# Dilated attention: four heads' scores in one piece, with the transposes and values of older steps, between the products of a fused three-block kernel

## The chip, the cores and the metric

One core of one Trainium2 chip runs the whole program. The time is device time in microseconds of one execution; the runs of a kernel are given by their median. TensorE (PE, its weight loads PEld), VectorE (DVE), ScalarE (ACT), GpSimd (POOL) and SyncE (SP, which issues the DMAs) each have their own instruction stream and wait for one another by semaphores.

## The reference, cut to what matters

Three transformer-like blocks follow one another on 512 tokens of 1024 features, all in float32: a block with RWKV-7 and differential attention between two gated feed-forwards, a second block with a pooling mixer and a dilated attention, and a third with mLSTM, sparse attention and a convolutional feed-forward. The change touches only the dilated attention of the second block. For each of three dilations (1, 4 and 16, numbered 0 to 2) and sixteen heads of 64 features:

```
s = q @ k.T * 0.125 - slope(dilation, head) * distance     # only keys in the window
m, z = max(s), sum(exp(s - m));  o = exp(s - m) @ v
out = merge of the three (o, m, z) by their maxima, divided by the merged z
out = out * silu(x @ w_gate), then @ w_out, residual, layer norm
```

In dilation 0 a query tile of 128 tokens sees its own and the preceding 128 keys (the first tile only its own). In the others the tokens are permuted, and each tile of 128 sees its own 128 keys.

## The kernel before, in words

Products with weights are done in three parts for accuracy: weights and activations are split into a high and a low float32r part, and `mm3` (L591) issues low x high, high x low, high x high (L594 to L596). The weights come as a stream of blocks of 128 x 512 (`Stream`, L152): SP loads a block, ScalarE casts its high part (L183), VectorE subtracts for the low part (L184). There are seven buffers for prepared blocks.

`dilated_heads` (L1500) loops over dilation `g` and a group `q` of four heads. Each turn computes keys and queries, `kq`: four columns of 8 k-steps, 512 tokens wide (`gemm_fg`, 32 steps of one `mm3`), and then values, `v`: four tiles of tokens, 8 k-steps of 256 columns each (`gemm_tg`, 16 steps of two `mm3`). These products go to three accumulator banks of PSUM (`acc`) and are copied out by ScalarE (L1517, L1523). In the first turn there is nothing beside them.

The attention of the group just projected is a generator, `dil_unit` (L1535), whose pieces end at a `yield`. `weave` (L145) runs the next turn's 48 product steps and lets the unit go one piece further after every `1 / pace` of them. So a unit's instructions stand between the next group's products on TensorE: `DIL_PACE` 0.5 gives its 24 pieces one place after every second step. The last unit stands beside the first 32 steps of the gate products (`gt`, `GATE_PACE` 0.8).

A unit has eight steps: four query tiles `i` times two pairs of heads `hp`. For each, three pieces:

- `scores` (L1553): for the two heads `b` of the pair a matmul of 64 rows (head `b` on partitions 64b to 64b+63) into a PSUM bank of its own (L1562); VectorE adds the bias and reduces the maximum (`mx`) on its way to `ds` (L1563), ScalarE exponentiates and sums (L1564).
- `turn` (L1567): TensorE transposes the exponentials in blocks of 128 x 128 into a third bank (L1574), and ScalarE or VectorE copies them to `dpT` (L933, L931).
- `values` (L1579): matmuls of 128 rows and 64 columns into the one bank `dO` (L1589); after two tiles `merge` (L1593) copies them out (dilation 0) or merges them with `dl_acc` by VectorE and POOL.

The order issued is scores of step n+1, turn of n, values of n. Scores, transposes and the like share four PSUM banks (`aux`) in turn. A float32 matmul leaves two records on TensorE for scores and values, and one for a transpose. At its end a dilation-0 unit is written to memory and read back in the permuted order by two DMAs of SP. The instructions of each engine are placed by the framework's scheduler, which keeps the issued order unless an instruction's buffers fall free earlier or later.

Of the kernel before, what the change touches and what calls it, by code (L numbers as in the profile page):

```python
# [9 lines left out]
F32 = mybir.dt.float32  # L10
F32R = mybir.dt.float32r
AF = mybir.ActivationFunctionType
ALU = mybir.AluOpType
# [3 lines left out]
P = 128  # L17
T = 512
# [45 lines left out]
LA_MORE = 6  # L64
WO_MORE = 3
KQ_FS = 4
DIL_PACE = 0.5
GATE_PACE = 0.8
GATE_LAG = 6
MEMSET = 8  # L70
PREP_PACE = 1.5
# [45 lines left out]
def chain(*gens):  # L117
    for g in gens:
        yield from g
# [25 lines left out]
def weave(main, other, n):  # L145

    fill(main, other, n)
    for _ in other:
        pass
# [234 lines left out]
class DiffAttention:  # L384
# [36 lines left out]
    def attend(self, d):  # L421
# [11 lines left out]
        def scores(n, m):  # L433
            i, h = todo[n]
            id, N = f"{d}_{i}_{h}", (i + 1) * P
            if m == 0:
# [77 lines left out]
class Build:  # L514
# [985 lines left out]
    def dilated_heads(self, u, up, accs, last):  # L1500
        nc, tc = self.nc, self.tc
        S = nc.scalar
        with tc.tile_pool(name="dil", bufs=1) as pd, tc.tile_pool(name="dild", bufs=4, space=bass.MemoryType.DRAM) as pdr:
            c = self.load_consts(pd, "cst2b", ["rel0", "rel1", "rel2"], self.ext["cst2"][:, 64:])
            perm = lambda a: a.rearrange("q (j p) -> q p j", p=4)

            def reorder(k, src, dst):
                nc.gpsimd.tensor_copy(dst[:, k].rearrange("q (p j) -> q p j", p=4), perm(src[:, k]))

            unit = None  # L1510
            for g in range(3):
                for q in range(4):
                    kq = pd.tile([P, 4, T], F32, tag="kq", bufs=2, name=f"kq{g}_{q}")
                    vt = pd.tile([P, 4, 256], F32, tag="vt", bufs=2, name=f"vt{g}_{q}")

                    def evac(n, ps, c0, c1, kq=kq):
                        S.copy(kq[:, n, c0:c1], ps)  # L1517

                    h0 = g * D + q * 256
                    cols = [("w_kv_2", h0), ("w_kv_2", h0 + P), ("w_in_b_2", h0), ("w_in_b_2", h0 + P)]  # L1520
                    ug = up if g else u
                    kqs = self.gemm_fg(ug, KD, cols, evac, fs=KQ_FS if g == q == 0 else 0, uid=f"kq{g}{q}")
                    vs = self.gemm_tg(ug, KD, "w_kv_2", 3 * D + h0, 256, lambda t, n, ps, vt=vt: S.copy(vt[:, t], ps), f"v{g}{q}")  # L1523
                    if not unit:
                        for _ in kqs:
                            pass
                        self.psum(**MIX_BANKS)
                        unit = iter(())
                        pairs = [(k, a, b) for a, b in ((u.hi, up.hi), (u.lo, up.lo)) for k in range(KD)]
                        self.steps(0, REORDER_GAP, [lambda x=x: reorder(*x) for x in pairs])  # L1530
                    weave(chain(kqs, vs), unit, DIL_PACE)
                    unit = self.dil_unit(g, q, kq, vt, accs[q], c, pd, pdr)
            weave(last, unit, GATE_PACE)

    def dil_unit(self, g, q, kq, vt, acc, c, pd, pdr):  # L1535
        nc = self.nc
        V, S, G = nc.vector, nc.scalar, nc.gpsimd
        mm = nc.tensor.matmul
        W = 256 if g == 0 else P
        rel = c[f"rel{g}"]  # L1540
        bias = pd.tile([P, 4, 256], F32, tag="dbias", bufs=2, name=f"dbias{g}_{q}")
        for h in range(4):
            slope = 2.0 ** (-8.0 * (g * 16 + q * 4 + h + 1) / 48.0)
            G.tensor_scalar(bias[:, h, :W], rel, -8.0 * slope, 0.0, op0=ALU.mult, op1=ALU.add)
        mx = pd.tile([P, 4, 4], F32, tag="dmx", bufs=2, name=f"dmx{g}_{q}")
        zz = pd.tile([P, 4, 4], F32, tag="dzz", bufs=2, name=f"dzz{g}_{q}")
        nat = None
        if g == 0:
            nat = pd.tile([P, 4, 264], F32, tag="dnat", bufs=1, name=f"dnat{q}")
        steps = [(i, hp) for i in range(4) for hp in range(2)]  # L1550
        st, po = {}, {}

        def scores(i, hp):  # L1553
            id = f"{g}{q}_{i}{hp}"
            N = P if (g or i == 0) else 256
            ks = slice(P * i, P * (i + 1)) if N == P else slice(P * (i - 1), P * (i + 1))
            s = pd.tile([P, 2, 256], F32, tag="ds", bufs=2, name=f"ds{id}")
            for b in range(2):
                h = 2 * hp + b
                ps = self.aux(f"dS{id}_{b}", N)  # L1560
                bs = slice(64 * b, 64 * b + 64)
                mm(ps, kq[bs, 2 + hp, P * i : P * (i + 1)], kq[bs, hp, ks], start=True, stop=True)  # L1562
                V.tensor_tensor_reduce(s[:, b, :N], ps, bias[:, h, W - N : W], -0.125, 3e38, ALU.add, ALU.min, mx[:, i, h : h + 1])  # L1563
                S.activation(s[:, b, :N], s[:, b, :N], AF.Exp, bias=mx[:, i, h : h + 1], scale=-1.0, accum_out=zz[:, i, h : h + 1])  # L1564
            st[i, hp] = (s, N)

        def turn(i, hp):  # L1567
            id = f"{g}{q}_{i}{hp}"
            s, N = st[i, hp]
            nb = N // P  # L1570
            pt = self.aux(f"dP{id}", 2 * N)
            for b in range(2):
                for j in range(nb):
                    nc.tensor.transpose(pt[:, (b * nb + j) * P : (b * nb + j + 1) * P], s[:, b, j * P : (j + 1) * P], self.ident)  # L1574
            pT = pd.tile([P, 512], F32, tag="dpT", bufs=2, name=f"dpT{id}")
            self.copy(i + hp, pT[:, : 2 * N], pt)
            st[i, hp] = pT, N

        def values(i, hp):  # L1579
            id = f"{g}{q}_{i}{hp}"  # L1580
            pT, N = st.pop((i, hp))
            nb = N // P
            if (i % 2, hp) == (0, 0):
                po[0] = self.po([P, 2, 4, 64], f"dO{id}")
            for b in range(2):
                h = 2 * hp + b
                for j in range(nb):
                    kt = i if N == P else i - 1 + j
                    mm(po[0][:, i % 2, h], pT[:, (b * nb + j) * P : (b * nb + j + 1) * P], vt[:, kt, h * 64 : (h + 1) * 64], start=j == 0, stop=j == nb - 1)  # L1589
            if (i % 2, hp) == (1, 1):  # L1590
                merge(i - 1, po[0])

        def merge(i0, po):  # L1593
            sl = slice(i0, i0 + 2)
            if g == 0:
                S.copy(nat[:, sl, :256], po.rearrange("a i h e -> a i (h e)"))
                return
            id = f"{g}{q}_{i0}"
            M, Z = acc[:, sl, 256:260], acc[:, sl, 260:264]
            t = pd.tile([P, 3, 2, 4], F32, tag="dmt", bufs=2, name=f"dmt{id}")  # L1600
            V.tensor_tensor(t[:, 0], M, mx[:, sl], op=ALU.min)
            V.tensor_tensor(t[:, 1], t[:, 0], M, op=ALU.subtract)
            V.tensor_tensor(t[:, 2], t[:, 0], mx[:, sl], op=ALU.subtract)
            S.activation(t[:, 1:], t[:, 1:], AF.Exp)
            V.tensor_copy(M, t[:, 0])
            V.tensor_tensor(Z, Z, t[:, 1], op=ALU.mult)
            V.tensor_tensor(zz[:, sl], zz[:, sl], t[:, 2], op=ALU.mult)
            V.tensor_tensor(Z, Z, zz[:, sl], op=ALU.add)
            for j in range(2):
                o = acc[:, i0 + j, :256].rearrange("a (h e) -> a h e", h=4)  # L1610
                bc = lambda a: a.unsqueeze(2).to_broadcast([P, 4, 64])
                V.tensor_tensor(o, o, bc(t[:, 1, j]), op=ALU.mult)
                w = pd.tile([P, 4, 64], F32, tag="dmw", bufs=2, name=f"dmw{id}_{j}")
                V.tensor_tensor(w, po[:, j], bc(t[:, 2, j]), op=ALU.mult)
                G.tensor_tensor(o, o, w, op=ALU.add)

        scores(*steps[0])
        yield
        for n, s in enumerate(steps):
            if n + 1 < len(steps):  # L1620
                scores(*steps[n + 1])
                yield
            turn(*s)
            yield
            values(*s)
            yield
        if g == 0:
            G.tensor_copy(nat[:, :, 256:260], mx)
            G.tensor_copy(nat[:, :, 260:264], zz)
            dr = pdr.tile([T, 264], F32, tag="dperm", name=f"dperm{q}")  # L1630
            nc.sync.dma_start(dr.rearrange("(i a) c -> a i c", a=P), nat)
            nc.sync.dma_start(acc, dr.rearrange("(j p) c -> j p c", p=4))

    def bias_rows(self, pool):

# [565 lines left out]
```

## Time and profile before

| | us |
|---|---|
| median of 3 runs (2902.62 to 2905.06) | 2902.79 |
| the profiled execution | 2904.9 |
| its span, first to last instruction | 2903.1 |
| TensorE busy | 2841.8 |
| VectorE / ScalarE / POOL busy | 1550.4 / 1211.3 / 431.5 |
| scores L1562 with the first unit's, from 1578.8 to | 2136.0 |

In a row of the profile `dS<-kq` names what is written and read, `64*128 64x256` the rows and columns of the array and then the shape, and "idle ... <-X" the time in which the engine stood still and what ended it. A matmul's recorded length holds its passage through the array, so the next one starts before it ends; what a matmul costs is read from start to start. A timeline joins equal neighbours of one engine to one row with a count; it starts at the first and is as long as to the last one's end.

### The profile page before, as it was taken

The page shows a single profiled execution, that of the slowest core. Times are in us where ns is not written, and L with a number is a line of the kernel's source. Part 1 is how long each engine was busy: PE and PEld are TensorE (multiplying, and loading weights), DVE is VectorE, ACT ScalarE, POOL GpSimd, SP SyncE. Part 2 cuts the span into 40 slices and gives each one's busy share as a digit, 9 for nine tenths or more (in the row PEclk, how much of TensorE's full clock was granted, in tenths as well). Part 3 has the DMA queues.
Part 4 walks back from the last instruction along what each step waited for, and adds up shares of the span by engine and source line. Part 5 has one row for each costly group of instructions (what it writes and reads, how often), then busy time and mean ns, then how long its engine had stood idle before and what let it go on. Part 6 is the DMA issues. An engine that isn't in the chain of part 4 may idle for free.

```text
span 2903.1 us, 44178 instructions
## 1 busy us (share of the span) xinstructions
PE 2841.8 (98%) x16743; PEld 2384.7 (82%) x16743; DVE 1550.4 (53%) x3365; ACT 1211.3 (42%) x2524; POOL 431.5 (15%) x509
## 2 busy tenths in 40 slices
PE   8999989999999999999999999999999999999998
PEld 7888887868887888888888888888899777888887
DVE  5443276565665443265446333444466895577742
ACT  5333263233334333243334444444474546554431
POOL 2110041010023110112304000111004023200001
PEclk9999999999999999999999999999999999999999
DMA  4333351101023333333242323222232421133332
GB/s 141 98 95 97 96 164 37 39 28 37 30 71 89 98 97 96 91 106 92 87 131 62 99 77 96 66 81 73 66 100 73 107 70 60 58 109 95 98 95 73
DMA packets 136141, 245.31 MB, mean 84 GB/s; under 512 B 15064, under 2 KB 22232, under 8 KB 135800
## 3 DMA queue, kind: packets, MB, share of 16 engines
q1 hardware_dynamic: 135928, 242.49, 27.6%
q8 instruction: 131, 2.15, 0.3%
q14 instruction: 82, 0.67, 0.1%
HBM read 235.75 MB, written 6.68 MB: 84 GB/s over the span
## 4 chain that ended last, share of the span: by engine, by line
PE 88%; DVE 6%; POOL 2%; ACT 2%; issue 1%; DMA 0%; SPq 0%; POOLq 0%; DVEq 0%; ACTq 0%
PE f_gu L594 5%; PE f_gu L596 5%; PE f_gu L595 5%; PE kq L594 3%; PE kq L595 3%; PE kq L596 3%; PE cf L594 3%; PE cf L595 3%; PE cf L596 3%; PE f L594 3%; PE f L596 3%; PE f L595 3%; PE v L594 2%; PE dO L1589 2%; PE v L595 2%; PE v L596 2%
## 5 line engine op out<-in xcount | busy, mean ns | idle before, releaser
L184 DVE TENSOR_TENSOR wlo<-wraw,whi 128x512 fp32r<-128x512 f32 (+1 forms) x858 | 627.2, 736 | 626.0 <-ACT whi L183 624.4
L183 ACT CAST whi<-wraw 128x512 fp32r<-128x512 f32 (+1 forms) x858 | 528.2, 619 | 897.1 <-PE f_gu L596 275.0
L594 PE MATMUL f<-f_ah,wlo 128*128 128x512 f32 (+1 forms) x440 | 153.8, 350 | 1.1 <-DVE wlo L184 1.1
L596 PE MATMUL f<-f_ah,whi 128*128 128x512 f32 (+1 forms) x440 | 153.4, 349 | 0.0
L595 PE MATMUL f<-f_al,whi 128*128 128x512 f32 (+1 forms) x440 | 153.4, 349 | 0.0
L594 PE MATMUL f_gu<-n_uh,wlo 128*128 128x512 f32 (+1 forms) x376 | 143.1, 381 | 9.2 <-ACT n_uh L788 8.2
L595 PE MATMUL f_gu<-n_ul,whi 128*128 128x512 f32 (+1 forms) x376 | 142.8, 380 | 0.0
L596 PE MATMUL f_gu<-n_uh,whi 128*128 128x512 f32 (+1 forms) x376 | 142.6, 379 | 0.0
L594 PE MATMUL f_gu<-won_uh,wlo 128*128 128x512 f32 (+1 forms) x376 | 142.2, 378 | 0.0
L596 PE MATMUL f_gu<-won_uh,whi 128*128 128x512 f32 (+1 forms) x376 | 142.0, 378 | 0.0
L595 PE MATMUL f_gu<-won_ul,whi 128*128 128x512 f32 (+1 forms) x376 | 141.8, 377 | 0.0
L594 PE MATMUL cf<-w3on_uh,wlo 128*128 128x512 f32 (+1 forms) x376 | 141.6, 377 | 0.0
L595 PE MATMUL cf<-w3on_ul,whi 128*128 128x512 f32 (+1 forms) x376 | 141.3, 376 | 0.0
L596 PE MATMUL cf<-w3on_uh,whi 128*128 128x512 f32 (+1 forms) x376 | 141.3, 376 | 0.0
L1563 DVE CUSTOM_DVE_ANT_0 ds<-dS,dbias 128x128 f32<-128x128 f32 (+1 forms) x192 | 54.9, 321 | 135.6 <-PE dS L1562 135.6
L1564 ACT ACTIVATE ds<-ds,dmx 128x128 f32<-128x128 f32 (+1 forms) x192 | 80.9, 422 | 100.7 <-DVE dmx L1563 100.3
L594 PE MATMUL kq<-dl_uh,wlo 128*128 128x512 f32 x256 | 112.6, 440 | 0.0
L595 PE MATMUL kq<-dl_ul,whi 128*128 128x512 f32 x256 | 100.7, 393 | 0.0
L596 PE MATMUL kq<-dl_uh,whi 128*128 128x512 f32 x256 | 100.2, 391 | 0.0
L594 PEld LDWEIGHTS f<-f_ah,wlo 128*128 128x128 f32 x440 | 82.7, 188 | 13.3 <-DVE wlo L184 1.3
L596 PEld LDWEIGHTS f<-f_ah,whi 128*128 128x128 f32 x440 | 82.7, 188 | 12.2
L595 PEld LDWEIGHTS f<-f_al,whi 128*128 128x128 f32 x440 | 82.7, 188 | 12.2
(831 smaller groups left out, 7606.0 us busy)
## 6 DMA issues: line engine op xcount, KB each, us to landing
wraw<-w SPq DMA_DIRECT2D x856, 256.0 KB, 2.6
dperm<-dnat SPq DMA_DIRECT2D x4, 528.0 KB, 3.9
dl_acc<-dperm SPq DMA_DIRECT2D x4, 528.0 KB, 3.6
x<-x SPq DMA_DIRECT2D x4, 512.0 KB, 6.9
xd<-x SPq DMA_DIRECT2D x8, 256.0 KB, 3.3
x<-xd SPq DMA_DIRECT2D x8, 256.0 KB, 3.6
toep<-rvd SPq DMA_DIRECT2D x8, 256.0 KB, 4.9
out<-x SPq DMA_DIRECT2D x16, 128.0 KB, 1.8
```

The costliest lines, as they stand in the source:

```text
L183: b.nc.scalar.copy(hi[:, s], raw[:, s])
L184: b.nc.vector.tensor_tensor(lo[:, s], raw[:, s], hi[:, s].bitcast(F32), op=ALU.subtract)
L594: mm(ps, a[1], b[0], start=start, stop=False)
L595: mm(ps, a[0], b[1], start=False, stop=False)
L596: mm(ps, a[0], b[0], start=False, stop=stop)
L1563: V.tensor_tensor_reduce(s[:, b, :N], ps, bias[:, h, W - N : W], -0.125, 3e38, ALU.add, ALU.min, mx[:, i, h : h + 1])
L1564: S.activation(s[:, b, :N], s[:, b, :N], AF.Exp, bias=mx[:, i, h : h + 1], scale=-1.0, accum_out=zz[:, i, h : h + 1])
L1589: mm(po[0][:, i % 2, h], pT[:, (b * nb + j) * P : (b * nb + j + 1) * P], vt[:, kt, h * 64 : (h + 1) * 64], start=j == 0, stop=j == nb - 1)
```

## The change

`scores` now takes all four heads of its tiles: one query tile in dilation 0, two in the others, so that a unit has 4 or 2 steps. Head `b` of both pairs and both tiles goes to bank `b`, at the columns that `slots` gives; all matmuls come first, then the reductions and exponentials. `turn` transposes a step's exponentials into two banks, one copied by ScalarE and one by VectorE. A piece consists of `turn` of step n-1, `values` of step n-2 and `scores` of step n, without a product in between: 5 pieces a unit in dilation 0, 3 in the others. A unit's last values, and in dilation 0 its write to memory, are handed on (`before`) and run in the next unit's first piece, ahead of its scores. The pace is set so that the pieces come after steps 10, 19, 28, 37 and 46 of 48, or 16, 31 and 46; beside the gates after 7, 14, 21 and, for the last values, 28 of 32. The buffers `ds` and `dpT` hold 2 x 512 columns in place of 2 x 256 and 512.

```diff
-DIL_PACE = 0.5
-GATE_PACE = 0.8
+DIL_STEPS = 46
+GATE_STEPS = 28
...
-                    weave(chain(kqs, vs), unit, DIL_PACE)
-                    unit = self.dil_unit(g, q, kq, vt, accs[q], c, pd, pdr)
-            weave(last, unit, GATE_PACE)
+                    weave(chain(kqs, vs), unit, pace)
+                    unit = self.dil_unit(g, q, kq, vt, accs[q], c, pd, pdr, before)
+                    pace = (3 if g else 5) / DIL_STEPS
+            weave(last, chain(unit, (f() for f in before)), 4 / GATE_STEPS)
...
-        steps = [(i, hp) for i in range(4) for hp in range(2)]
+        steps = [(i,) for i in range(4)] if g == 0 else [(0, 1), (2, 3)]
...
+        def slots(tiles):
+            return [(i, hp, (hp * len(tiles) + j) * 512 // (2 * len(tiles))) for hp in range(2) for j, i in enumerate(tiles)]
+
+        def scores(n):
+            tiles = steps[n]
...
+            N = P if (g or n == 0) else 256
+            s = pd.tile([P, 2, 512], F32, tag="ds", bufs=2, name=f"ds{id}")
+            ps = [self.aux(f"dS{id}_{b}") for b in range(2)]
+            for i, hp, a in slots(tiles):
+                ks = slice(P * i, P * (i + 1)) if N == P else slice(P * (i - 1), P * (i + 1))
+                for b in range(2):
+                    bs = slice(64 * b, 64 * b + 64)
+                    mm(ps[b][:, a : a + N], kq[bs, 2 + hp, P * i : P * (i + 1)], kq[bs, hp, ks], start=True, stop=True)
             for b in range(2):
...
+                for i, hp, a in slots(tiles):
+                    h = 2 * hp + b
+                    o = s[:, b, a : a + N]
+                    V.tensor_tensor_reduce(o, ps[b][:, a : a + N], bias[:, h, W - N : W], -0.125, 3e38, ALU.add, ALU.min, mx[:, i, h : h + 1])
+                    S.activation(o, o, AF.Exp, bias=mx[:, i, h : h + 1], scale=-1.0, accum_out=zz[:, i, h : h + 1])
...
+        def turn(n):
...
+            pT = pd.tile([P, 2, 512], F32, tag="dpT", bufs=2, name=f"dpT{id}")
+            for b in range(2):
+                pt = self.aux(f"dP{id}_{b}")
+                for _, _, a in slots(steps[n]):
+                    for c0 in range(a, a + N, P):
+                        nc.tensor.transpose(pt[:, c0 : c0 + P], s[:, b, c0 : c0 + P], self.ident)
+                if N * 2 * len(steps[n]) == 512:
+                    self.copy(b, pT[:, b], pt)
...
+        for n in range(L + 1):
+            if n:
+                turn(n - 1)
+            if n >= 2:
+                values(n - 2)
+            if not n and before:
+                before[0]()
+            if n < L:
+                scores(n)
+            if n == L:
+                before[:] = [finish]
             yield
```

## Rows read from the trace of the kernel before

**Rows 1.** The page, first part: busy us (share of the span) and instructions.
```profile
PE 2841.8 (98%) x16743; PEld 2384.7 (82%) x16743; DVE 1550.4 (53%) x3365; ACT 1211.3 (42%) x2524; POOL 431.5 (15%) x509
```
**Rows 2.** One window: length; PE, PEld, DVE, ACT, POOL busy (count); clock, DMA share, GB/s.
```profile
1802.00:2108.00 306.00, 306.00 (x1901) 255.33 (x1901) 132.50 (x501) 134.24 (x406) 29.50 (x50) 1.00 0.25 76
```
**Rows 3.** Waits, 1602 to 2145 us, of PE and then of PEld: total, times, longest.
```profile
PE dO L1589 <- ACT dpT L933: 0.3, 1, 0.3
...
PEld dS L1562 <- issue: 23.8, 66, 0.4
```
**Rows 4.** The tile dS: duration ns min/median/max, first and last start, forms.
```profile
L1562 PE MATMUL dS<-kq x384: 271/373/481, 1578.8 to 2136.0; 64*128 64x128 f32 x144, 64*128 64x256 f32 x48
L1563 DVE CUSTOM_DVE_ANT_0 ds<-dS,dbias x192: 276/292/426, 1580.3 to 2136.6; 128x128 f32<-128x128 f32 x144, 128x256 f32<-128x256 f32 x48
```
**Rows 5.** Timeline of PE (start, length): scores of 128 keys in `kq` products.
```profile
1854.25 0.39 PE L595 MATMUL kq<-dl_ul,whi 128*128 128x512 f32 x1
1854.48 0.40 PE L596 MATMUL kq<-dl_uh,whi 128*128 128x512 f32 x1
1854.81 0.49 PE L1562 MATMUL dS<-kq 64*128 64x128 f32 x4
...
1855.57 0.39 PE L595 MATMUL kq<-dl_ul,whi 128*128 128x512 f32 x1
```
**Rows 6.** Timeline of PE: scores of 256 keys in `v` products.
```profile
1645.14 0.28 PE L595 MATMUL v<-wlo,lan_uh 128*128 128x256 f32 x1
1645.26 0.28 PE L596 MATMUL v<-whi,lan_uh 128*128 128x256 f32 x1
1645.47 0.70 PE L1562 MATMUL dS<-kq 64*128 64x256 f32 x4
...
1646.32 0.28 PE L595 MATMUL v<-wlo,lan_uh 128*128 128x256 f32 x1
```
**Rows 7.** Timelines cut within those two pieces, to 1854.85, 1855.0 and (two) 1645.6.
```profile
1854.81 0.19 PEld L1562 LDWEIGHTS dS<-kq 64*128 64x128 f32 x2 [0.37 <-issue]
...
1854.81 0.30 PEld L1562 LDWEIGHTS dS<-kq 64*128 64x128 f32 x4 [0.37 <-issue]
...
1645.46 0.30 PEld L1562 LDWEIGHTS dS<-kq 64*128 64x128 f32 x4
...
1645.47 0.49 PE L1562 MATMUL dS<-kq 64*128 64x256 f32 x2
```
**Rows 8.** Timeline of PE: two transposes in `kq`, eight value matmuls in `v`.
```profile
1851.04 0.39 PE L596 MATMUL kq<-dl_uh,whi 128*128 128x512 f32 x1
1851.27 0.38 PE L1574 MATMUL dP<-ident,ds 128*128 128x128 f32 x2
...
1851.72 0.40 PE L595 MATMUL kq<-dl_ul,whi 128*128 128x512 f32 x1
...
1642.93 0.28 PE L596 MATMUL v<-whi,lan_uh 128*128 128x256 f32 x1
1643.05 1.00 PE L1589 MATMUL dO<-vt,dpT 128*128 128x64 f32 x8
...
1644.06 0.28 PE L595 MATMUL v<-wlo,lan_uh 128*128 128x256 f32 x1
```
**Rows 9.** Timeline of ACT, 1831 to 1846.5 us (a `v` stretch): the weight casts.
```profile
1831.56 0.62 ACT L183 CAST whi<-wraw 128x512 fp32r<-128x512 f32 x1
...
1843.29 1.33 ACT L183 CAST whi<-wraw 128x512 fp32r<-128x512 f32 x2 [0.80 <-PE v L596]
...
1844.92 0.62 ACT L183 CAST whi<-wraw 128x512 fp32r<-128x512 f32 x1
...
1845.90 0.62 ACT L183 CAST whi<-wraw 128x512 fp32r<-128x512 f32 x1
```
**Rows 10.** The line L1564: duration ns min/median/max.
```profile
L1564 ACT ACTIVATE ds<-ds,dmx x192: 385/402/512, 1587.6 to 2137.8; 128x128 f32<-128x128 f32 x144, 128x256 f32<-128x256 f32 x48
...
L1564 ACT ACT_TABLE_LOAD x5: 1283/1283/1283, 1586.3 to 2136.1; - x5
```

More of the change, by code (lines that the diff above doesn't have):

```diff
@@ L1508, in reorder @@
                 nc.gpsimd.tensor_copy(dst[:, k].rearrange("q (p j) -> q p j", p=4), perm(src[:, k]))
-            unit = None
+            unit, before, pace = None, [], 0
             for g in range(3):
@@ L1530, in dilated_heads, with dil_unit @@
                         self.steps(0, REORDER_GAP, [lambda x=x: reorder(*x) for x in pairs])
-                    weave(chain(kqs, vs), unit, DIL_PACE)
-                    unit = self.dil_unit(g, q, kq, vt, accs[q], c, pd, pdr)
-            weave(last, unit, GATE_PACE)
-    def dil_unit(self, g, q, kq, vt, acc, c, pd, pdr):
+                    weave(chain(kqs, vs), unit, pace)
+                    unit = self.dil_unit(g, q, kq, vt, accs[q], c, pd, pdr, before)
+                    pace = (3 if g else 5) / DIL_STEPS
+            weave(last, chain(unit, (f() for f in before)), 4 / GATE_STEPS)
+    def dil_unit(self, g, q, kq, vt, acc, c, pd, pdr, before):
         nc = self.nc
@@ L1549, in dil_unit @@
             nat = pd.tile([P, 4, 264], F32, tag="dnat", bufs=1, name=f"dnat{q}")
-        steps = [(i, hp) for i in range(4) for hp in range(2)]
+        steps = [(i,) for i in range(4)] if g == 0 else [(0, 1), (2, 3)]
         st, po = {}, {}
[L1553 to L1557, printed above, removed]
-            for b in range(2):
[L1559 to L1565, printed above, removed]
@@ L1567, in turn @@
-        def turn(i, hp):
-            id = f"{g}{q}_{i}{hp}"
-            s, N = st[i, hp]
-            nb = N // P
[L1571 to L1583, printed above, removed]
-                po[0] = self.po([P, 2, 4, 64], f"dO{id}")
[L1585 to L1591, printed above, removed]
+        def slots(tiles):
+            return [(i, hp, (hp * len(tiles) + j) * 512 // (2 * len(tiles))) for hp in range(2) for j, i in enumerate(tiles)]
@@ new lines, in scores @@
+        def scores(n):
+            tiles = steps[n]
+            id = f"{g}{q}_{n}"
+            N = P if (g or n == 0) else 256
[6 more added lines that the diff above has]
+                    mm(ps[b][:, a : a + N], kq[bs, 2 + hp, P * i : P * (i + 1)], kq[bs, hp, ks], start=True, stop=True)
+            for b in range(2):
+                for i, hp, a in slots(tiles):
[3 more added lines that the diff above has]
+                    S.activation(o, o, AF.Exp, bias=mx[:, i, h : h + 1], scale=-1.0, accum_out=zz[:, i, h : h + 1])
+            st[n] = (s, N)
@@ new lines, in turn @@
+        def turn(n):
+            id = f"{g}{q}_{n}"
+            s, N = st[n]
+            pT = pd.tile([P, 2, 512], F32, tag="dpT", bufs=2, name=f"dpT{id}")
[6 more added lines that the diff above has]
+                    self.copy(b, pT[:, b], pt)
+                else:
+                    sp = lambda x: x.rearrange("p (h n) -> p h n", h=2)[:, :, :N]
+                    self.copy(b, sp(pT[:, b]), sp(pt))
+            st[n] = pT, N
@@ new lines, in values @@
+        def values(n):
+            id = f"{g}{q}_{n}"
+            pT, N = st.pop(n)
+            nb = N // P
+            if steps[n][0] % 2 == 0:
+                po[0] = self.po([P, 2, 4, 64], f"dO{id}")
+            for i, hp, a in slots(steps[n]):
+                for b in range(2):
+                    h = 2 * hp + b
+                    for j in range(nb):
+                        kt = i if N == P else i - 1 + j
+                        mm(po[0][:, i % 2, h], pT[:, b, a + j * P : a + (j + 1) * P], vt[:, kt, h * 64 : (h + 1) * 64], start=j == 0, stop=j == nb - 1)
+            if steps[n][-1] % 2:
+                merge(steps[n][-1] - 1, po[0])
@@ L1615, in merge, with finish @@
                 G.tensor_tensor(o, o, w, op=ALU.add)
[L1617 to L1623, printed above, removed]
-            yield
[L1625 to L1632, printed above, removed]
+        L = len(steps)
+        def finish():
+            values(L - 1)
+            if g == 0:
+                G.tensor_copy(nat[:, :, 256:260], mx)
+                G.tensor_copy(nat[:, :, 260:264], zz)
+                dr = pdr.tile([T, 264], F32, tag="dperm", name=f"dperm{q}")
+                nc.sync.dma_start(dr.rearrange("(i a) c -> a i c", a=P), nat)
+                nc.sync.dma_start(acc, dr.rearrange("(j p) c -> j p c", p=4))
+        for n in range(L + 1):
[9 more added lines that the diff above has]
+                before[:] = [finish]
+            yield
     def bias_rows(self, pool):
```

## The prediction

> **What bounds the kernel now.** I read the page first: TensorE is busy for 2841.8 of 2903.1 us, VectorE for half of it [rows 1]. Then the windows of the dilated stage: in the 306 us in which seven units of dilations 1 and 2 run beside products TensorE is busy all the time, while VectorE and ScalarE work 132 and 134 us, and the granted clock is full, its level of 2.4 GHz [rows 2]. Then the waits of TensorE between 1602 and 2145 us: its matmuls waited for another engine for 0.3 us in all. Its weight loads, however, stood still for 23.8 us ahead of `dS`, 66 times, with "issue" as the reason: they waited for nothing that the profile names [rows 3]. So this stage ends when TensorE's own instructions end, and what counts is what an inserted piece costs TensorE beyond the products around it. I read that cost from the timeline. Take the start of the last product before a piece and the start of the second product after it, and take off two ordinary steps (the first product after a piece has its start modelled early, so the second one is used).
>
> **The scores as they stand.** There are 384 score matmul records and 192 reductions, one reduction a head and tile: 144 of 128 keys and 48 of 256 [rows 4]. A piece holds two heads, so there are 96 pieces: 72 of 128 keys and 24 of 256. One of 128 keys between `kq` products: 1855.57 - 1854.48 = 1.09 us, less two steps of 0.23 (1854.48 - 1854.25) is 0.63 us [rows 5]. One of 256 keys between `v` products: 1646.32 - 1645.26 = 1.06, less two steps of 0.12, is 0.82 us [rows 6].
>
> What is in the 0.63? The score matmuls use 64 rows, head b on rows 64b to 64b+63. Two of the loads finish within 0.19 us, about the length of one: they run side by side, one on each half of the array. All four finish within 0.30 us, so the second pair starts 0.11 us behind the first [rows 7]. I call such a pair a slot: 0.11 us for 128 columns, two slots a piece. 256 columns add 0.82 - 0.63 = 0.19 to two slots, so a slot of 256 takes about 0.21 us. What is left is fixed: 0.63 - 0.22 = 0.41, and 0.82 - 0.42 = 0.40. It lies at the two edges. The first score load starts at 1854.81, 0.33 us after the last product, where a product would have followed after 0.23; no weight is loaded ahead there, and the same happens on the way back to 128 rows (the 0.37 us of idle load in the row is this) [rows 7]. So entering and leaving the 64-row scores costs some 0.40 us whatever number of heads stands between.
>
> **Scores in one piece.** With the change a piece holds four heads. In dilation 0 it holds one query tile: 4 units x 4 pieces, of which 4 have 128 keys and 12 have 256, four slots each. In the other two it holds two tiles: 8 units x 2 pieces of 128 keys, eight slots each. That is 32 pieces in place of 96; the slots are the same ones.
> Before: 72 x 0.63 + 24 x 0.82 = 65.0 us.
> After: 16 x 8 x 0.11 = 14.1, 4 x 4 x 0.11 = 1.8, 12 x 4 x 0.21 = 10.1, edges 32 x 0.40 = 12.8, sum 38.7 us.
> Gain: 26.3 us, which is 64 edges of 0.41. The lower bound is worked out under the second rival; the upper one is the whole 96 x 0.40 = 38 us, if a long piece hid its edges, for which no row speaks.
>
> **Transposes and values.** Their counts stay. Do they have an edge too? Two transposes between `kq` products: 1851.72 - 1851.04 - 0.46 = 0.22 us, 0.11 each. Eight value matmuls between `v` products: 1644.06 - 1642.93 - 0.24 = 0.89, 0.11 each [rows 8]. A burst of two and a burst of eight cost the same per instruction, so these have no edge (they are 128-row matmuls like the products), and gathering the 192 pieces saves nothing. I take 0; the rounding of 0.01 us a burst bounds it to 2 us either way.
>
> **What the pieces wait for.** Before, transposes come 8 product steps after their scores and values 2 steps after the transposes. After, each comes one piece later, which is 9 steps in dilation 0 and 15 in the others. The shortest way is dilation 0 in `kq` steps: 9 x 3 x 0.23 = 6.2 us. In that time VectorE must reduce four heads and ScalarE run four exponentials. An exponential takes ScalarE 0.40 us [rows 10], 0.51 at most, so four take 2.0 and the eight of a two-tile piece 3.2 us, the latter against 15 x 0.69 = 10.4 us. Covered. The products' copies out of PSUM stand behind those exponentials on ScalarE: three accumulator banks, each reused 3 columns (16 us) or 3 tokens (8.6 us) later, against a hold of 3.2 us. Covered. The four small banks alternate: transposes take two, scores the other two, and each pair rests for a whole piece. If that cover went, one wait would cost up to the 3.2 us of the exponentials.
> The thin place is the end. The last unit runs beside the gate products, its pieces 7 steps of 0.72 = 5.0 us apart, and ScalarE there also swaps between the exponential's table and another, 1.28 us a load, five times [rows 10]: 3.2 + 1.28 + 0.6 for a cast is about the 5.0. I put 0.5 us on it (0 to 3).
> A unit's last values, and the DMA that writes a finished dilation-0 unit out and back, move into the next unit's first piece, 10 to 16 steps later. The results are needed a whole dilation (some 190 us) later, so SP's and POOL's queues have room; 0. The last unit's last merge is issued at step 28 of 32 rather than 30, so what follows isn't later.
>
> **Sum.** The profiled execution took 2904.9 us, 1.8 more than its span. 2904.9 - 26.3 + 0.5 = 2879.1. The median shown, 2902.79, is 2.1 below the profiled one, so the median after should be 2877.
>
> **Rivals.**
> 1. ScalarE's queue. Eight exponentials at once (3.2 us) stand ahead of the weight casts. At step 31, one step before `v` starts, the first scores are through after some 2.5 us, ScalarE is free at 5.7, copies a column (taken as long as a cast, 0.6) and only then casts `v`'s third block (0.62): ready at 6.9, its low half, taken as long again, at 7.5. TensorE wants it after 0.88 (transposes) + 1.29 (scores) + 0.69 (step 32) + 1.44 (`v`'s first two blocks) = 4.3. That is a wait of 3.2 us at 7 changes from `kq` to `v`, 22 us, and most of the gain is gone: 2899. Against it: the casts are not made when a block becomes current. At the change at 1831 only one is made, and four come together when the end of `v` lets go of its blocks [rows 9]. So the seven buffers are kept full, and `v`'s blocks are cast while `kq` runs. Chance 0.07.
> 2. Loads in the open. In a long burst the third pair's load follows a pair on the same two halves. If it cannot hide behind the multiplication there, part of what I call edge is really slot: 0.22 us for 128 columns and 0.32 for 256, and the edge is 0.63 - 0.44 = 0.19. The gain is then 64 x 0.19 = 12 us: 2891. Against it: in the piece of 256 keys the four loads are through at 1645.46 + 0.30 = 1645.76, while the first pair's matmuls run to 1645.96 [rows 7], so the second pair was loaded beside them. Chance 0.10.
> The Trainium skill (TensorE: Matmul & The Clock Gate, Part 3: Packing small matmuls, The mechanism) says that a weight load overlaps running matmuls only where its row group differs. By it this rival would hold and the sum would be 2891; the row on the 256-key piece speaks against it, for one pair deep.
> 3. The pairs fall apart, the slower side. If in a burst over two tiles the two halves no longer run side by side, and each instruction loads and multiplies in turn, 288 x 0.22 + 96 x 0.32 + 32 x 0.19 = 100 us stand against 65: 35 us slower, 2938. It turns slower as soon as an instruction costs over (65.0 - 32 x 0.19) / 384 = 0.15 us on average. The order stays head b=0, b=1, tile after tile, which is what gives pairs today, and the halves write two banks as now. Chance 0.04.
> 4. It doesn't do what it says: the instructions are placed by a scheduler, not in the order of issue alone (the casts of [rows 9] stand where buffers fall free). If it lets products into the long pieces, most edges stay and the time is 2895 to 2903. Chance 0.04.
>
> **How the numbers follow.** The forecast has 0.75, and by itself 2874 to 2880 (edge 0.39 to 0.42, waits 0 to 3). 2871 to 2891 also takes in rival 2 and the 2 us of the transposes and values; rivals 1, 3 and 4, 0.15, stay out. A measurement here tells 0.2% (5.8 us) from no change. Faster: 0.75 + 0.10 + half of rival 4 = 0.87. Same: rival 1 and the rest of rival 4, 0.09. Slower: rival 3, 0.04.
>
> **What would show it.** Scores in bursts of 8 and 16 records, 32 of them; the second product after a burst of 16 comes 0.41 + 0.88 = 1.29 us later than two steps (1.95 by rival 2, 3.7 by rival 3); idle loads ahead of `dS` about a third of 23.8 us; transposes and values still 0.11 us each; no new row of several us among TensorE's waits. A wait of `v` for a cast or of `dP` for `ds` over 5 us in sum, or a stage from the first `kq` of dilation 1 to the gates that is not some 17 us shorter (7 units, 6 edges of 0.41 each), would make the prediction wrong.

## The result, and the profile after

The changed kernel takes 2876.7 us (median of 4 runs, 2875.5 to 2878.4), the kernel before beside it 2903.9 (4 runs). The ratio is 0.9906, 95% interval 0.9889 to 0.9923. The forecast was 2877, its range 2871 to 2891. The profiled execution took 2876.86 us, its span 2875.0, against 2904.9 and 2903.1.

The page has TensorE at 98% as before [rows 1], with 25.7 us less of busy time:

```profile
PE 2816.1 (98%) x16743; PEld 2390.0 (83%) x16743; DVE 1544.8 (54%) x3349; ACT 1194.8 (42%) x2504; POOL 430.6 (15%) x509
```

The window of the same seven units, from the first `kq` product of dilation 1's second unit to the first gate product, is 288.30 us long. Before, it went from 1802.02 to 2108.52, 306.50 us [rows 2, cut at whole us]. TensorE is busy throughout, at the full granted clock, as it was; so the 18.2 us come from its own instructions. The columns are those of [rows 2]:

```profile
1791.44:2079.74 288.30, 288.30 (x1906) 256.52 (x1905) 130.09 (x486) 127.68 (x394) 27.09 (x49) 1.00 0.27 82
```

The waits of TensorE and, below, of its weight loads from 1602 to 2150 us (the answer to [rows 3]): total, times, longest. The idle ahead of `dS` is a tenth of the 23.8 us. New is the wait of `gT`, the gates' transposes, for the merge of the last unit (`dl_y`); the last line is the kernel before, 1602 to 2180 us, where `gT` waited for `gsg` alone:

```profile
PE gT L1483 <- DVE dl_y L1487: 2.3, 3, 1.7
PE gT L1483 <- DVE gsg L1477: 0.3, 1, 0.3
...
PEld kq L594 <- issue: 2.6, 8, 0.3
PEld dS L1570 <- issue: 2.4, 13, 0.4
...
PE gT L1483 <- DVE gsg L1477: 1.2, 3, 0.5
```

The tile `dS` has the records and reductions of [rows 4], so the work is the same:

```profile
L1570 PE MATMUL dS<-kq x384: 272/272/480, 1578.0 to 2095.2; 64*128 64x128 f32 x144, 64*128 64x256 f32 x48
L1575 DVE CUSTOM_DVE_ANT_0 ds<-dS,dbias x192: 277/286/426, 1612.0 to 2098.0; 128x128 f32<-128x128 f32 x144, 128x256 f32<-128x256 f32 x48
```

The timeline of PE (start, length) shows two of the new pieces among `kq` products. In the first, eight transposes and sixteen scores: 1859.38 - 1856.76 = 2.62 us, less two steps of 0.23, is 2.16; 0.88 of it are the transposes (8 x 0.11), 1.28 the scores. In the second, sixteen values and sixteen scores: 1888.07 - 1884.58 - 0.46 = 3.03; 1.79 are the values, 1.24 the scores. Seven pieces of each kind in `kq` differ among themselves by no more than 0.001 us:

```profile
1856.76 0.39 PE L596 MATMUL kq<-dl_uh,whi 128*128 128x512 f32 x1
1856.99 1.03 PE L1587 MATMUL dP<-ident,ds 128*128 128x128 f32 x8
1857.95 1.16 PE L1570 MATMUL dS<-kq 64*128 64x128 f32 x16
1859.05 0.50 PE L594 MATMUL kq<-dl_uh,wlo 128*128 128x512 f32 x1
1859.38 0.39 PE L595 MATMUL kq<-dl_ul,whi 128*128 128x512 f32 x1
...
1884.58 0.40 PE L596 MATMUL kq<-dl_uh,whi 128*128 128x512 f32 x1
1884.81 1.89 PE L1606 MATMUL dO<-vt,dpT 128*128 128x64 f32 x16
1886.63 1.16 PE L1570 MATMUL dS<-kq 64*128 64x128 f32 x16
1887.72 0.50 PE L594 MATMUL kq<-dl_uh,wlo 128*128 128x512 f32 x1
1888.07 0.40 PE L595 MATMUL kq<-dl_ul,whi 128*128 128x512 f32 x1
```

**Where the time went.** I did this sum (second product after a piece, less the last before it, less two steps) for every piece of the stage. I call the total the pieces' cost. It is 146.7 us before and 119.5 after, 27.2 less. Such a total shifts by up to 1 us with the way in which a step is taken (with the median step the difference is 26.7).

The profiled executions differ by 28.0 us. Of that, 0.9 was there before the stage began (the first `la_b` product starts at 1544.01 before and 1543.12 after). The waits of `gT` grew from 1.2 to 2.6 us and gave 1.4 back. Some 1.4 came from product steps that the sum doesn't see: outside the pieces a `kq` step takes 0.231 us on average before and 0.229 after. The first gate product comes 28.8 us earlier (2108.52 to 2079.74), but 1.8 of that only moved behind it: sixteen value records that now stand beside the gates. The last gate product comes 28.4 earlier, and after it little changes (`aS`, 300 us on, is 28.2 earlier).

### The profile page after: what moved, and what is told of

It reads as the page before. It is cut to its first block, busy times and chain, and to the rows that moved or that the text cites. A ratio compares the mean times of both kernels' runs of the same rounds, so it can differ in the third digit from the quotient of the medians.

```text
span 2875.0 us, 44121 instructions
## 1 busy us (share of the span) xinstructions
PE 2816.1 (98%) x16743; PEld 2390.0 (83%) x16743; DVE 1544.8 (54%) x3349; ACT 1194.8 (42%) x2504; POOL 430.6 (15%) x509
## 4 chain that ended last, share of the span: by engine, by line
PE 87%; DVE 6%; ACT 2%; POOL 2%; issue 1%; DMA 1%; SPq 0%; POOLq 0%; DVEq 0%; ACTq 0%
PE f_gu L594 5%; PE f_gu L596 5%; PE f_gu L595 5%; PE kq L594 3%; PE kq L595 3%; PE kq L596 3%; PE cf L596 3%; PE cf L595 3%; PE cf L594 3%; PE f L594 3%; PE f L595 3%; PE f L596 3%; PE dO L1606 2%; PE v L594 2%; PE v L596 2%; PE v L595 2%
## 5 line engine op out<-in xcount | busy, mean ns | idle before, releaser
L594 PE MATMUL kq<-dl_uh,wlo 128*128 128x512 f32 x256 | 101.9, 398 | 0.0
L596 PEld LDWEIGHTS f<-f_ah,whi 128*128 128x128 f32 x440 | 82.6, 188 | 12.2
L594 PEld LDWEIGHTS f_gu<-n_uh,wlo 128*128 128x128 f32 x376 | 71.9, 192 | 21.3 <-ACT n_uh L788 7.3
```

What stands on the lines that cost most here:

```text
L594: mm(ps, a[1], b[0], start=start, stop=False)
L596: mm(ps, a[0], b[0], start=False, stop=stop)
```

## The experiments

Theory: a burst of 64-row scores costs TensorE a fixed 0.41 us for going from 128 rows to 64 and back, whatever stands in it, plus a slot of 0.11 or 0.21 us for each pair of records; only the number of bursts counts. The rivals are told with each run. All were timed in five rounds with the kernel before on the same chip. Runs 1 to 4 shared one chip (before: 2906.0), runs 6 to 9 another (before: 2904.7), and run 5 came last, beside its own comparison (before: 2904.9).

**1. The transposes, values and scores apart, the scores still four heads together.**

```
+        if more:
+            more = next(filler, None) == "more"
+            continue
...
             if n:
                 turn(n - 1)
+                yield "more"
             if n >= 2:
                 values(n - 2)
+                if n < L:
+                    yield "more"
...
```

> The changed kernel, but transposes, values and scores of a piece stand apart again, one product step between each; scores stay together for four heads (32 bursts of scores, some 95 inserted bursts in all). Theory (the gain is 64 edges into and out of the 64-row scores): only the slightly cheaper way from values straight to scores is lost, 19 x 0.05 = 1 us: 2878, 26 us below the kernel before. Rival (the gain comes from having 44 bursts between the products in place of 288, 0.11 us for each one fewer): 51 of those 244 return, 5.6 us: 2882.

It took 2877.6 us (4 runs), ratio 0.9900 (0.9887 to 0.9914): 28.4 below the kernel before, where theory had 26 and the rival some 22. The pieces' cost is 120.5 in 99 bursts, where the changed kernel has 119.5 in 46. The timeline of PE has the sixteen scores alone: 2057.93 - 2056.18 - 0.46 = 1.29 us, the 0.41 + 0.88 of the forecast to 0.01:

```profile
2056.18 0.39 PE L599 MATMUL kq<-dl_uh,whi 128*128 128x512 f32 x1
2056.50 1.16 PE L1573 MATMUL dS<-kq 64*128 64x128 f32 x16
2057.59 0.50 PE L597 MATMUL kq<-dl_uh,wlo 128*128 128x512 f32 x1
2057.93 0.39 PE L598 MATMUL kq<-dl_ul,whi 128*128 128x512 f32 x1
```

So standing transposes and values beside the scores is worth about 1 us of the 27: transposes and values have no edge of their own. Scores directly behind values are 0.05 us cheaper than behind a product (1.24 against 1.29), and there are 19 such pieces.

**2. Each score burst cut in two by one product step.**

```
                     mm(ps[b][:, a : a + N], kq[bs, 2 + hp, P * i : P * (i + 1)], kq[bs, hp, ks], start=True, stop=True)
+                if hp == 0 and i == tiles[-1]:
+                    yield "more"
...
-                scores(n)
+                yield from scores(n)
```

> The changed kernel, but each burst of scores is cut in two, one pair of heads before and one after a product step; all else stays joined. Theory: 32 edges of 0.41 return, 13 us: 2890; the second part of a burst costs 0.41 us beyond its slots. Rival (number of bursts): 32 of 244 return, 3.5 us: 2880.

It took 2890.0 us (5 runs), ratio 0.9945 (0.9932 to 0.9957). That is 16.0 below the kernel before, where the changed kernel is 27.2 below (28.6 in run 9): 11 to 13 us are lost, as theory had it, not 3.5. The pieces' cost is 131.7, 12.2 more than after, for 32 more bursts: 0.38 each. A second half of eight records alone costs 0.85. The loads' idle ahead of `dS` comes back (1602 to 2145 us):

```profile
PEld dS L1573 <- issue: 11.9, 39, 0.4
```

With bursts of 4, 8 and 16 records of 128 columns alone (0.62 in the median of the kernel before, 0.85 here, 1.29 in run 1) the cost is a straight line: 0.11 a pair of records and 0.40 at its foot.

**3. The reverse: the two-head scores of before, but with transposes and values in the same piece.**

```
-DIL_PACE = 0.5
-GATE_PACE = 0.8
+DIL_PACE = 10 / 46
+GATE_PACE = 10 / 28
...
-        scores(*steps[0])
-        yield
-        for n, s in enumerate(steps):
...
+        for n in range(L + 2):
+            if 1 <= n <= L:
+                turn(*steps[n - 1])
+            if n < L:
+                scores(*steps[n])
+            if n >= 2:
+                values(*steps[n - 2])
...
+            yield
```

> The kernel before with scores of two heads a piece as it was (96 bursts of scores), but transposes, scores and values of a piece without products between them (10 pieces a unit, 120 in all, in place of 24 and 288). Theory: 96 edges as before, so no gain: 2901 to 2904. Rival (number of bursts): 168 of 244 parts of the gain, 18 us: 2885.

It took 2904.2 us (11 runs), ratio 0.9993 (0.9984 to 1.0002): no difference that can be told. The pieces' cost is 146.7, that of the kernel before within the 1 us of this sum, though pieces that had been apart now touch. The 96 score bursts remained, and that is what counts. Gathering pieces is worth nothing where it does not lower the number of score bursts.

**4. The kernel before, piece for piece, with scores over 128 rows.** Each head's queries stand beside 64 rows of zeros, so two heads' keys may be loaded whole and the result is the same.

```
+            qzs = [pd.tile([P, 4, T], F32, name=f"qz{j}") for j in range(2)]
+            for qz in qzs:
+                for h in range(4):
+                    z = 64 * (1 - h % 2)
+                    nc.gpsimd.memset(qz[z : z + 64, h], 0.0)
...
+                            S.copy(qz[bs, 2 * (n - 2) + b, c0:c1], ps[bs])
...
-                mm(ps, kq[bs, 2 + hp, P * i : P * (i + 1)], kq[bs, hp, ks], start=True, stop=True)
+                mm(ps, qz[:, h, P * i : P * (i + 1)], kq[:, hp, ks], start=True, stop=True)
```

> The kernel before, piece for piece, but the scores use all 128 rows: each head's queries stand in a tile of their own whose other 64 rows are zero, so a matmul of 128 rows gives the same scores. Nothing runs side by side any more and ScalarE copies each query column in two halves of 64 partitions. Theory (the edge comes from going from 128 to 64 rows and back): no edge is left, 288 x 0.11 + 96 x 0.21 = 52 us of scores in place of 65: 13 us faster than before, 2891, and a score burst costs 0.44 us (128 keys) or 0.85 (256 keys) beyond the products. Rival (the edge comes with any float32 score burst, its banks or its semaphores): 52 + 96 x 0.4 = 90 us, 25 us slower, 2929.

It took 2901.1 us (11 runs), ratio 0.9982 (0.9973 to 0.9991): 4.9 us less, and 13 were expected. The scores did cost what theory said: the 96 bursts fell from 65.1 to 52.9 us. Two side effects of the edit took most of it back. Each copy of query columns on ScalarE became two, and values now wait for the `dpT` that ScalarE copies. The fills on GpSimd stood ahead of its part of the additions of `lav_sqacc`, which began 1.5 us later; VectorE's part waited for that, and `lav_s` waited 4.6 us for VectorE (2.0 in the kernel before). These are the waits of PE from 1560 to 1602 us and of its loads from 1602 to 2145:

```profile
PE lav_s L758 <- DVE lav_sqacc L724: 4.6, 1, 4.6
...
PEld dO L1600 <- ACT dpT L933: 5.8, 12, 0.5
```

After that wait the granted clock was 0.50, the lower level of 1.2 GHz, in the next 4.2 us; ahead of it TensorE had done 0.34 us of work in 4.8. The windows show it (length; PE, PEld, DVE, ACT, POOL busy; clock):

```profile
1570.00:1574.80 4.80, 0.34 (x3) 0.14 (x2) 1.99 (x6) 2.17 (x5) 3.02 (x6) 0.78 0.00 0
1574.80:1579.00 4.20, 4.11 (x19) 4.14 (x20) 1.40 (x3) 0.62 (x1) 0.71 (x1) 0.50 0.23 62
```

**5. The same without the two side effects** (run last; the edit is shown against run 4): VectorE copies the second half of the queries, and it writes the zeros too, from the first two units' accumulators.

```
-            for qz in qzs:
-                for h in range(4):
-                    z = 64 * (1 - h % 2)
-                    nc.gpsimd.memset(qz[z : z + 64, h], 0.0)
...
-                            S.copy(qz[bs, 2 * (n - 2) + b, c0:c1], ps[bs])
+                            self.copy(b, qz[bs, 2 * (n - 2) + b, c0:c1], ps[bs])
+                            if new:
+                                nc.vector.tensor_scalar(qz[bs, 2 * (n - 2) + 1 - b, c0:c1], ps[bs], 0.0, None, op0=ALU.mult)
```

> The kernel before, piece for piece, with scores over 128 rows again (each head's queries stand beside 64 rows of zeros), without the two side effects of the earlier run: no GpSimd fill at the stage's start (the zeros are written by VectorE from the first two units' accumulators) and the second half of the query columns is copied by VectorE, not ScalarE. Theory: the edge belongs to the change between 64 and 128 rows, so the 96 score bursts still cost 12 us less in sum than before, and now the kernel is 10 to 12 us faster than before on the same chip (about 2893). Rival A, the edge is a cost of any burst, and the earlier 12 us are paid back elsewhere whatever starts the stage: within 5 us of before. Rival B, the copies on VectorE delay its reductions and TensorE waits for ds or dpT by as much: 3 to 6 us of new waits, 6 to 9 us faster.

It took 2895.0 us (6 runs), ratio 0.9966 (0.9954 to 0.9978), which is 9.9 us less than before, 6 to 13 by the interval. Theory's 10 to 12 lies in it, though so does the upper part of rival B, but B's waits are not there: from 1602 to 2145 us the loads waited 0.4 us for `dpT` and 0.2 for `ds` (0.5 and 0.2 in the kernel before), none stood idle ahead of `dS`, and `lav_s` waited 1.9 us (2.0 in the kernel before). Rival A (within 5 us) falls. The pieces' cost is 134.3, 12.4 less than before. The timeline of PE has a burst of four among `kq` products: 1893.33 - 1892.41 - 0.46 = 0.46 us here, 0.445 in the median, four times 0.11, where [rows 5] have 0.63:

```profile
1892.41 0.40 PE L596 MATMUL kq<-dl_uh,whi 128*128 128x512 f32 x1
1892.64 0.61 PE L1571 MATMUL dS<-kq,qz 128*128 128x128 f32 x4
1893.01 0.48 PE L594 MATMUL kq<-dl_uh,wlo 128*128 128x512 f32 x1
1893.33 0.39 PE L595 MATMUL kq<-dl_ul,whi 128*128 128x512 f32 x1
```

So the edge belongs to the change between 128 rows and the 64-row pairs, and goes where the rows stay 128; what within that change takes the time, no run shows. There each record has a slot to itself: with 256 columns four cost 0.86, more than two slots and an edge (0.83). This form therefore gains less than the longer burst does.

**6. Longer still: scores over four banks,** two query tiles a burst in dilation 0 and four in the others, 16 bursts. The transposes stand in a piece of their own, and `ds` and `dpT` are kept once.

```
-        steps = [(i,) for i in range(4)] if g == 0 else [(0, 1), (2, 3)]
+        steps = [(0, 1), (2, 3)] if g == 0 else [(0, 1, 2, 3)]
...
-            ps = [self.aux(f"dS{id}_{b}") for b in range(2)]
+            pss = [self.aux(f"dS{id}_{b}") for b in range(4)]
```

> The changed kernel with scores over four PSUM banks, one a head: two query tiles a burst in dilation 0, all four in the others, so 16 bursts of scores in place of 32; transposes likewise over four banks in a piece of their own; the buffers of exponentials and transposes once in place of twice, so no memory is added. Theory (0.40 us an edge): 16 x 0.40 = 6.4 us below the changed kernel beside it, some 35 us below the kernel before. Rival (what was left after 32 bursts is hidden elsewhere, or sixteen exponentials in a row, 6.4 us of ScalarE, hold the transposes or the weight casts): no gain, or waits of transposes for exponentials of 1 us and more.

It took 2870.8 us (4 runs), ratio 0.9880 (0.9866 to 0.9893); the changed kernel took 2876.2 beside it (run 9). It beats both kernels, the changed one by 5.3 us. The pieces' cost is 113.1, just 6.4 below, 16 edges of 0.40; `gT` waits 2.6 us for `dl_y` (1.6 in run 9, 2.3 in the changed kernel's first profile), about what 5.3 lacks of 6.4. The timeline of PE: 1843.13 - 1838.75 - 0.46 = 3.92 us, 0.89 more than the 3.03 with half the scores, eight slots of 0.11:

```profile
1838.75 0.40 PE L596 MATMUL kq<-dl_uh,whi 128*128 128x512 f32 x1
1838.98 1.89 PE L1613 MATMUL dO<-vt,dpT 128*128 128x64 f32 x16
1840.81 2.06 PE L1573 MATMUL dS<-kq 64*128 64x128 f32 x32
1842.79 0.50 PE L594 MATMUL kq<-dl_uh,wlo 128*128 128x512 f32 x1
1843.13 0.40 PE L595 MATMUL kq<-dl_ul,whi 128*128 128x512 f32 x1
```

**7. The changed kernel with its pieces three product steps apart,** so that transposes follow their scores closely.

```
-                    pace = (3 if g else 5) / DIL_STEPS
+                    pace = 1 / 3
```

> The changed kernel with its pieces 3 product steps (2.1 us) apart, not 9 or 15; the unit beside the gates unchanged. Tests that the distance, not chance, covers the exponentials. Theory: eight exponentials need 3.2 us and some 0.8 ahead of them, the next transposes stand 2.1 us behind: the scheduler then places scores between the transposes where it finds them late, three more edges of 0.41 in each of 8 two-tile units or first units, 10 us, and TensorE waits another 0.5 to 1.5 us at each of 14 second pieces: 2890 to 2908 by the scale of 2877. Rival (the exponentials never mattered): 2877.

It took 2896.8 us (6 runs), ratio 0.9971 (0.9959 to 0.9982), 20.6 more than the changed kernel beside it; the pieces' cost is 137.0. Three things add up to about the loss. First, the exponentials are late, and the scheduler fills the gaps between transposes with scores. That is a form of rival 4 of the prediction, though scores and not products part the piece. Eight pieces have four score bursts in place of one, 24 edges or 9.6 us at 0.40. The timeline of PE shows one of seven such pieces: 1889.55 - 1885.46 - 0.46 = 3.63 us, where the changed kernel takes 2.16:

```profile
1885.46 0.40 PE L596 MATMUL kq<-dl_uh,whi 128*128 128x512 f32 x1
1885.70 0.71 PE L1587 MATMUL dP<-ident,ds 128*128 128x128 f32 x5
1886.34 0.49 PE L1570 MATMUL dS<-kq 64*128 64x128 f32 x2
1886.75 0.33 PE L1587 MATMUL dP<-ident,ds 128*128 128x128 f32 x1
1887.01 0.48 PE L1570 MATMUL dS<-kq 64*128 64x128 f32 x2
...
1888.36 0.93 PE L1570 MATMUL dS<-kq 64*128 64x128 f32 x10
1889.22 0.50 PE L594 MATMUL kq<-dl_uh,wlo 128*128 128x512 f32 x1
1889.55 0.39 PE L595 MATMUL kq<-dl_ul,whi 128*128 128x512 f32 x1
```

Second, the loads waited, a quarter of the loss (1602 to 2145 us):

```profile
PEld dP L1587 <- ACT ds L1576: 4.9, 19, 0.4
```

Third, the granted clock fell to 0.50, the level of 1.2 GHz, twice in the stage, for 10.2 us in sum. It did not fall between 1602 and 2080 us in either profile of the changed kernel. The mean granted clock of all six executions was 0.991 to 0.994, of run 9's four 0.994 to 0.996, so the profiled one is no exception. By an estimate from these rows that costs up to half of the 10.2, 5.1 us. TensorE had been busy for 3.40 of the 3.64 us before the first fall; why the clock fell is open. The columns are those of the windows of run 4:

```profile
2014.00:2017.64 3.64, 3.40 (x14) 1.85 (x13) 1.59 (x14) 3.64 (x19) 0.00 (x0) 1.00 0.01 2
2017.64:2024.47 6.83, 6.83 (x26) 5.30 (x25) 4.65 (x27) 3.92 (x18) 1.66 (x4) 0.50 0.15 40
2065.43:2068.84 3.41, 3.41 (x13) 2.61 (x12) 3.41 (x24) 2.39 (x13) 0.00 (x0) 0.50 0.00 0
```

The three sum to 19.6 us, though they overlap in part. The time lies in the range of the forecast, which had the edges and larger waits but not the clock.

So the distance between pieces, which the prediction took as cover for a wait, also keeps the bursts whole.

**8. The changed kernel with the heads of a burst in another order:** all on the lower half of the array first, then all on the upper.

```
-            for i, hp, a in slots(tiles):
...
-                for b in range(2):
-                    bs = slice(64 * b, 64 * b + 64)
+            for b in range(2):
+                bs = slice(64 * b, 64 * b + 64)
+                for i, hp, a in slots(tiles):
```

> The changed kernel with the score matmuls of a burst in another order: all of the heads b=0 (rows 0 to 63), then all of b=1 (rows 64 to 127), so neighbours no longer use different halves of the array; same bursts, same edges. Theory: what pairs them is the order; one after the other each record costs a slot, 0.11 us (128 keys) or 0.21 (256), so 144 x 0.11 + 48 x 0.21 = 26 us come back: about 2903. If weights cannot be loaded beside a multiplication on the same half, each record costs 0.22 or 0.32 and the time is some 2938. Rival (the two halves find each other whatever the order): 2877.

It took 2883.8 us (5 runs), ratio 0.9928 (0.9915 to 0.9940), 7.6 more than the changed kernel. All three expectations missed. The timeline of PE gives a piece with sixteen scores 1847.22 - 1843.19 - 0.46 = 3.57 us, 0.54 more than after:

```profile
1843.19 0.40 PE L596 MATMUL kq<-dl_uh,whi 128*128 128x512 f32 x1
1843.42 1.89 PE L1606 MATMUL dO<-vt,dpT 128*128 128x64 f32 x16
1845.24 1.71 PE L1570 MATMUL dS<-kq 64*128 64x128 f32 x16
1846.88 0.50 PE L594 MATMUL kq<-dl_uh,wlo 128*128 128x512 f32 x1
1847.22 0.39 PE L595 MATMUL kq<-dl_ul,whi 128*128 128x512 f32 x1
...
1845.24 0.93 PE L1570 MATMUL dS<-kq 64*128 64x128 f32 x6
```

The last line is the same burst cut at 1845.81. The loads, cut at 1845.78 and 1845.81, show why:

```profile
1845.24 0.63 PEld L1570 LDWEIGHTS dS<-kq 64*128 64x128 f32 x5
...
1845.24 0.74 PEld L1570 LDWEIGHTS dS<-kq 64*128 64x128 f32 x7
```

Five loads on one half follow each other at 0.11 us ((0.63 - 0.19) / 4), each beside the multiplication of the one before. Then two start together: by the order of issue (the trace doesn't name the half) the sixth of the lower half and the first of the upper, which is the ninth in the list. So the second half starts three records ahead of its turn and no more: 5 records alone, 3 in pairs, 5 alone, 13 slots in place of 8, and 5 x 0.11 is the 0.54. The bursts of eight lose nothing (2.991 against 2.985 us for a whole piece); why not, is open.

**9. The changed kernel again,** as the mark for runs 6 to 8.

> The changed kernel again, unchanged, on the same chip as the three others, as their measure: 26 to 28 us below the kernel before.

It took 2876.2 us (4 runs), ratio 0.9896 (0.9881 to 0.9912), which is 28.6 below the kernel before where 26 to 28 were expected; its pieces' cost is 119.46, that of the first profile.

## Why the prediction was right

**The bound.** TensorE's own instructions set the stage's end, before and after. The pieces' cost fell by 27.2 us and the kernel by 28.0 in the profiled executions. That the median of 2877 was met to 0.3 us is luck: the forecast took 25.8 us off 2902.79, while the kernel before beside it took 2903.9 and 27.2 came off.

**The edge.** 0.40 to 0.41 us a burst held in bursts of 4, 8 and 16 (run 2). With 32 bursts more 11 to 13 us were lost, with 16 fewer 5 were won; with the same 96 in other pieces nothing changed, and without the change of rows the kernel before was 10 us faster. The forecast's 26.3 us came out as 27.2 (26.7 with median steps). The cheaper entry behind values, 19 x 0.05, is as large as the difference; [rows 5, 6] could not show it, since no score there stands behind values. That nothing else is in the difference isn't shown, as it lies within the 1 us of the sum.

**Slots.** 0.11 us a pair held up to 32 records. The cost of a burst of sixteen was 1.285 behind transposes, 1.24 behind values and 1.289 alone, forecast 1.29. Rival 2 asked 1.95, rival 3 3.7: both fall. The Trainium skill (TensorE: Matmul & The Clock Gate, Part 3: Packing small matmuls, The mechanism) says that a load overlaps running matmuls only where its row group differs; the same section also has loads for a background weight buffer pulled ahead of running matmuls. Run 8 decides against the first for this chip: five loads on one half, 0.19 us long, start 0.11 us apart while the records before them multiply on the same half. The kernel before spoke against it too: weight loads were busy for 82% of the span and matmuls for 98% [rows 1], most of them products that fill all 128 rows, so rival 2's 0.10 was high.

**Transposes and values.** Taken as 0, within 2 us; run 1 makes them 0 and the cheaper entry 1.

**Waits.** Taken as 0.5 us, 0 to 3; 1.4 were given back, so the size is in the bounds, but for another reason than the prediction gave. It feared the exponential behind a table load; `dP` waited 0.7 us for `ds` in all. What waits is `gT`, 2.3 us for `dl_y` (1.6 in run 9), while its wait for `gsg` shrank by 0.9. The last merge, which the prediction held to be no later by its product steps, is up to 1.7 us late for the gates.

**Marks that failed.** Idle loads ahead of `dS` were to be about a third of 23.8 us and are 2.4, while the edge is there 32 times. That row lists 13 of the 32. The prediction took the 0.37 us of idle load in [rows 7] for both edges, but it stands ahead of the first score load alone, and its size hangs on what comes before: 0.37 us behind a product, 0.17 behind transposes, 0.07 behind values, where the row lists nothing. It is a sign of the edge and not its size. The stretch from the first `kq` product of dilation 1 to the gates fell by 20.1 us (355.5 to 335.4), not by some 17: it holds an eighth unit, the last of dilation 0. The window of the seven units alone fell by 18.2.

**Rivals 1 and 4.** No wait of `v` for a cast appeared between 1602 and 2150 us. The scheduler left the long pieces whole at the change's distances; run 7 shows that this hangs on the distances.

## What to carry to other kernels

Where TensorE is the bound, price an inserted piece by the time between the products around it, less their own steps, and split that into what grows with the records and what does not; here bursts of 64-row matmuls among 128-row ones cost 0.40 us each, from 4 to 32 records long, so they are worth gathering, while 128-row transposes and values are not. Before gathering, see that the work which feeds the next piece stays further off than the engines need, or the scheduler can take the piece apart again. Padding a matmul with zero rows to the full 128 removes that cost too, but doubles its slots and needs someone to write the zeros.

## What was not expected of the hardware

In run 8 the upper half of the array began three records ahead of the order of issue and no more, so an interleaved order was worth 0.54 us in a burst of sixteen, and nothing in one of eight. A burst that follows values enters its 64 rows 0.05 us sooner than one that follows a product or a transpose.

In run 4 TensorE's wait of 4.6 us was followed by 4.2 us at 1.2 GHz, and the first `v` product came 3.8 us later than before, for 2.6 us more of waiting. But the length of the wait does not decide it alone: behind a wait of 1.95 us at the same place the clock stayed at 1.00 in the kernel before (first line, 29 records) and was 0.50 in the changed one (second line, 18 records). And in run 7 it fell while TensorE was busy.

```profile
1573.40:1576.80 3.40, 3.39 (x29) 3.40 (x30) 1.75 (x5) 1.31 (x3) 0.71 (x1) 1.00 0.26 77
1571.56:1574.97 3.41, 3.41 (x18) 3.41 (x18) 0.87 (x3) 0.62 (x1) 0.71 (x1) 0.50 0.25 79
```
